# Loads of the row tiles of x issued from GpSimd's queue in a cumsum-difference matmul

## The chip, the cores and the metric

One Trainium2 chip, one core. The metric is device time in microseconds (us). Before: 1450.54 us, the median of three runs from 1450.36 to 1450.79.

## What is computed

The reference takes x (8 batches x 2048 rows x 2048 columns, float32) and w (2048 x 2048, float32):

```python
cs = np.cumsum(x, axis=1)
diff = cs - np.concatenate([np.zeros(...), cs[:, :-1, :]], axis=1)
return np.matmul(diff, w).astype(np.float32)
```

The difference of a running sum is the input again, so the kernel computes x @ w, with 16384 rows of x.

## The kernel before

The rows of x are cut into 128 tiles of 128 rows. The first four tiles ("plain", `PLAIN = 4`) are multiplied in bf16 in the ordinary way while w is still arriving. Their x comes in through `load_x` (L249), on SyncE's queue. From tile 4 on, tiles are taken four at a time: two pairs, and a scheme of Strassen's kind with fewer products, in f16. Each such group of four is one period of the program; after the first of these groups (`group_plain`) there are 30 periods of the same pattern (`group`).

A tile beyond the plain ones goes through these steps, each recorded by its own helper:

- `load` (L125): two halves of 512 KB each from x into one of four staging buffers F (`stage`, a list used first in, first out). The DMA is at L132.
- `weigh_one` (L135): ScalarE sums the absolute values of each half (L140), to get a scale.
- `scale_of` (L152): ScalarE adds the two sums (L161), VectorE takes the reciprocal (L163), ScalarE makes the unit that undoes the scale (L167).
- `narrow_one` (L173): ScalarE casts the half to f16 with that scale (L178). The narrowed second half gives its buffer back.
- `turn_one` (L193): a DMA transpose of each narrowed half into `turned_x` (L195). After the second one the other buffer is given back.
- Then TensorE multiplies (L588 in `matmuls`, L610 in `quarter`), ScalarE and VectorE empty PSUM (L624, L627, L635), VectorE forms sums of tiles and of blocks of w (L576), and SyncE stores (L643, L655).

Names in the text below are the kernel's own labels. `load0.0` is the first half of the first tile beyond the plain ones, `load2.0` and `load2.1` the halves of the third, and so on; `weigh0.0`, `narrow0.0` and `turn0.0` are the same half's later steps. A role from 4 to 10 names a tile that is prepared in one period for the next ones. The second of these tiles (`load1`) is loaded by a function of its own, `load_5`, at L517.

Before the products in f16 can start, w is scaled. VectorE takes the largest absolute value of every block of w (L305) and of all of these (L447); GpSimd takes the largest over the partitions (`max of all`, PARTITION_ALL_REDUCE, L451); from that come `uw` and `uinv` (L453, L454), and with them VectorE and ScalarE make the f16 blocks `B11`, `B21`, `B22` of w (L460, L462).

**The order is written out by hand.** Every operation is recorded with a label and the engine whose queue it goes to, and at the end `emit` (L205) sorts all of them by a number from the table `places`. `after` (L98) ties each operation behind the one before it on the same engine's list:

```python
def after(engine, ask):
    if engine in last:
        with tc.issue_after(last[engine].ins):
            said = ask()
    ...
    last[engine] = said[-1] if isinstance(said, tuple) else said
```

In `places`, `max of all` has number 235 and `load0.0` number 458. Before the change `max of all` is the only operation on the list "pool". SyncE's list "sp" has 817 DMAs: loads of x and w, transposes and stores.

Of the kernel before, what the change touches and what calls it, by code (L numbers as in the profile page):

```python
# [10 lines left out]
def kernel(  # L11
# [6 lines left out]
    nc = tc.nc  # L18
    P = 128
# [6 lines left out]
    NH = N // 2  # L26
# [21 lines left out]
    x2 = x.rearrange("b s d -> (b s) d")  # L48
# [67 lines left out]
    def record(label, engine, ask):  # L116
        at = seen[period[0], label] = seen.get((period[0], label), 0) + 1
        if at > 1:
            label = f"{label}#{at}"
        ops.append((period[0], label, engine, ask))  # L120

    def role(t):
        return t - PLAIN - 4 * period[0]

    def load(t, i):  # L125
        if t < END:
            to = stage.pop(0)
            where.setdefault(t, [None, None])[i] = to
            record(
                f"load{role(t)}.{i}",  # L130
                "sp",
                lambda: nc.sync.dma_start(to, x2[ds(t * P, P), ds(i * NH, NH)]),  # L132
            )

    def weigh_one(t, i):  # L135
# [308 lines left out]
    for t in (PLAIN, PLAIN + 2):  # L444
        load(t, 0)
        load(t, 1)
# [86 lines left out]
    narrow(PLAIN + 1)  # L533
    turn(PLAIN + 1)
    load(PLAIN + 3, 0)
    load(PLAIN + 3, 1)

# [1045 lines left out]
```

## Time and profile before

| what | us |
|---|---|
| median of three runs | 1450.54 |
| span of the profiled execution, first to last instruction | 1449.2 |
| TensorE (PE) busy in it | 1438.6 |
| VectorE (DVE) busy | 1334.3 |
| ScalarE (ACT) busy | 1204.5 |
| GpSimd (POOL) busy | 0.5 |

The profiled execution is known by its span of 1449.2 us; the median of the timed runs is 1.3 us above it, the time around the first and last instruction. The span is one execution on the one core. A busy share is the time in which the engine worked on an instruction; SyncE's queue only issues DMAs and is not counted. Its entries are written SPq. The time of a DMA "to landing" runs from the start of its issue to the update of its semaphore.

### The profile page before, as it was taken

What the parts mean: (1) busy time and instruction counts of PE and PEld (TensorE: products, weight loads), DVE (VectorE), ACT (ScalarE), POOL (GpSimd) and SP (SyncE); (2) the same over time, 40 slices, a digit from 0 to 9 for tenths busy, and PEclk for the clock granted to TensorE, in tenths of its full rate; (3) what the DMA queues carried; (4) which work ended last, traced back from release to release, by engine and by line L of the source; (5) the groups of instructions that cost most, each with busy time, mean ns of one, the idle gap of its engine ahead of it and who ended that gap; (6) DMA issues with size and microseconds to landing.
All of it is one profiled execution on the core that took longest, in us unless ns stands there. A gap on an engine that the chain in (4) does not pass through costs nothing.

```text
span 1449.2 us, 20358 instructions
## 1 busy us (share of the span) xinstructions
PE 1438.6 (99%) x6692; PEld 652.2 (45%) x6698; DVE 1334.3 (92%) x2345; ACT 1204.5 (83%) x1994; POOL 0.5 (0%) x5
## 2 busy tenths in 40 slices
PE   8999999999999999999999999999999999999998
PEld 4444444444444444444444444444444444444443
DVE  6999999999999999999999999999999999999988
ACT  5997888898888888888988888988888888889783
POOL 0000000000000000000000000000000000000000
PEclk9999999999999999999999999999999999999999
DMA  9999979899888999989998888998989998989973
GB/s 360 369 252 272 252 212 228 240 247 262 226 234 226 243 262 231 244 222 228 247 265 233 228 229 237 252 257 226 222 239 244 260 248 225 218 236 248 264 200 116
DMA packets 343930, 351.59 MB, mean 243 GB/s; under 512 B 270992, under 2 KB 270992, under 8 KB 343824
## 3 DMA queue, kind: packets, MB, share of 16 engines
q1 hardware_dynamic: 343824, 350.29, 89.4%
q8 instruction: 52, 0.85, 0.2%
q14 instruction: 54, 0.44, 0.1%
HBM read 150.99 MB, written 134.22 MB: 197 GB/s over the span
## 4 chain that ended last, share of the span: by engine, by line
PE 91%; issue 4%; DMA 2%; ACT 2%; DVE 1%; DVEq 0%; POOLq 0%; ACTq 0%; SPq 0%
PE b L610 61%; PE b L588 30%; DMA x<-F 1%; DMA F<-in_x_dram 1%; DVE W L460 1%; ACT waste L140 0%; DMA out_dram<-arena 0%; ACT W L462 0%; DVE arena L635 0%; ACT arena L624 0%; ACT F L178 0%; ACT arena L342 0%; ACT arena L178 0%; DVE arena L576 0%; DVE W L576 0%
## 5 line engine op out<-in xcount | busy, mean ns | idle before, releaser
L588 PE MATMUL b<-W,x 128*128 128x512 f16 x2144 | 518.1, 379 | 0.1
L635 DVE SCALAR_TENSOR_TENSOR arena<-b,tiny,arena 128x512 f32<-128x512 f32 x612 | 446.9, 745 | 16.0 <-PE b L610 4.8
L610 PEld LDWEIGHTS <-arena 128*128 128x128 f16 x2744 | 268.2, 98 | 325.4 <-DVE arena L576 6.3
L610 PE MATMUL b<-W,arena 128*128 128x512 f16 x1672 | 413.7, 379 | 0.8 <-DVE arena L576 0.4
L624 ACT ACTIVATE arena<-b,tiny 128x512 f32<-128x512 f32 x496 | 317.0, 684 | 35.4 <-PE b L588 14.9
L588 PEld LDWEIGHTS <-x 128*128 128x128 f16 x2144 | 209.7, 98 | 253.3 <-issue 0.3
L140 ACT ACTIVATE waste<-F,tiny 128x1024 uint8<-128x1024 f32 x246 | 283.9, 1154 | 15.6 <-DMA F<-in_x_dram 14.1
L178 ACT ACTIVATE F<-F,tiny 128x1024 f16<-128x1024 f32 x246 | 282.1, 1147 | 10.9 <-DVE tiny L163 9.4
L610 PE MATMUL b<-W,x 128*128 128x512 f16 x1192 | 287.5, 379 | 0.0
L610 PE MATMUL b<-arena 128*128 128x512 f16 x1072 | 261.6, 379 | 0.0
L610 PEld LDWEIGHTS <-x 128*128 128x128 f16 x1428 | 139.7, 98 | 168.5
L576 DVE TENSOR_TENSOR b<-b,arena 128x512 f32<-128x512 f32 x298 | 205.9, 691 | 5.7 <-ACT arena L627 2.0
L627 ACT COPY b<-b 128x512 f32<-128x512 f32 x149 | 85.5, 574 | 134.4 <-PE b L610 112.4
L627 ACT COPY arena<-b 128x512 f32<-128x512 f32 x298 | 170.2, 580 | 19.9 <-PE b L610 13.0
L576 DVE TENSOR_TENSOR arena<-W 128x2048 f16<-128x2048 f16 (+1 forms) x158 | 185.6, 1176 | 0.4 <-PE b L610 0.4
L576 DVE TENSOR_TENSOR arena<-x,x 128x512 f16<-128x512 f16 (+1 forms) x181 | 91.5, 506 | 50.1 <-PE b L610 50.1
L576 DVE TENSOR_TENSOR x<-x,x 128x1024 f16<-128x1024 f16 x124 | 85.2, 687 | 2.0
L576 DVE TENSOR_TENSOR arena<-W,arena 128x512 f16<-128x512 f16 (+1 forms) x157 | 85.9, 563 | 0.6 <-PE b L610 0.5
L576 DVE TENSOR_TENSOR arena<-arena 128x512 f16<-128x512 f16 x120 | 50.8, 424 | 13.7 <-PE b L610 11.8
L610 PE MATMUL b<-arena,x 128*128 128x512 f16 x236 | 60.3, 379 | 0.0
L324 PE MATMUL b<-arena 128*128 128x512 bf16 x234 | 53.5, 379 | 1.5 <-DVE arena L279 0.8
L576 DVE TENSOR_TENSOR arena<-x,arena 128x512 f16<-128x512 f16 x119 | 49.6, 417 | 0.6 <-PE b L610 0.6
(49 smaller groups left out, 503.6 us busy)
## 6 DMA issues: line engine op xcount, KB each, us to landing
F<-in_x_dram SPq DMA_DIRECT2D x246, 512.0 KB, 5.4
out_dram<-arena SPq DMA_DIRECT2D x240, 512.0 KB, 4.8
W<-in_w_dram SPq DMA_DIRECT2D x31, 512.0 KB, 9.5
out_dram<-arena SPq DMA_DIRECT2D x31, 256.0 KB, 2.7
W<-in_x_dram SPq DMA_DIRECT2D x16, 256.0 KB, 6.6
x<-F SPq DMA_TRANSPOSE x246, 4.4
arena<-in_x_dram SPq DMA_DIRECT2D x2, 512.0 KB, 5.1
W<-in_w_dram SPq DMA_DIRECT2D x2, 256.0 KB, 9.0
```

The source lines that it names most:

```text
L140: lambda: nc.scalar.activation(waste, data, ABS, bias=least, scale=1.0 / ROW, accum_out=m),
L178: lambda: nc.scalar.activation(to, data, COPY, scale=s),
L324: said = nc.tensor.matmul(to[n], xP[:, r, ko, :], b[:, ds(n * NB, NB)], start=(ko == 0), stop=(ko == KO - 1),)
L460: ask = lambda: nc.vector.tensor_scalar(to, src, uinv, None, MUL)
L576: record(label, "dve", lambda: nc.vector.tensor_tensor(dst, p, q, op))
L588: said = nc.tensor.matmul(to[n], a[k], b[k][:, n, :], start=(start and k == 0), stop=(k == KH - 1), skip_group_check=True,)
L610: said = nc.tensor.matmul(to, a[k], b[k], start=(start and k == 0), stop=(k == 3), skip_group_check=True)
L624: record(label, "act", lambda: nc.scalar.activation(c, p, COPY, scale=u))
L627: record(label, "act", lambda: nc.scalar.copy(to, p))
L635: label, "dve", lambda: nc.vector.scalar_tensor_tensor(c, p, u, c, MUL, ADD)
```

## The change

The loads at L132 are recorded for the list "pool" and issued with `nc.gpsimd.dma_start`. Source, destination, size and number (246, of 512 KB) stay. `load_x`, `load_5`, the loads of w, the transposes and the stores stay on SyncE's queue. The numbers in `places` stay as well, so on GpSimd's list the 246 loads stand behind `max of all`, in the order they had among themselves.

```diff
@@ -128,8 +128,8 @@
             where.setdefault(t, [None, None])[i] = to
             record(
                 f"load{role(t)}.{i}",
-                "sp",
-                lambda: nc.sync.dma_start(to, x2[ds(t * P, P), ds(i * NH, NH)]),
+                "pool",
+                lambda: nc.gpsimd.dma_start(to, x2[ds(t * P, P), ds(i * NH, NH)]),
             )
```

## Prediction

> **What bounds the kernel now.** I read the page first, for busy times and the chain that ended last, then the table of windows for one round of the loop, then the timelines of the place where the order of GpSimd's list touches the chain.
>
> ```profile
> PE 1438.6 (99%) x6692; PEld 652.2 (45%) x6698; DVE 1334.3 (92%) x2345; ACT 1204.5 (83%) x1994; POOL 0.5 (0%) x5
> PE 91%; issue 4%; DMA 2%; ACT 2%; DVE 1%; DVEq 0%; POOLq 0%; ACTq 0%; SPq 0%
> ```
>
> ```profile
> 386.40 12.09 PE b L610 x56
> ...
> 430.43 12.09 PE b L610 x56
> ```
>
> ```profile
> 711.00:755.00 44.00, 44.00 (x206) 19.94 (x204) 40.71 (x73) 37.45 (x64) 0.00 (x0) 1.00 0.92 239
> ```
>
> The second block is the chain in order of time: the same piece returns after 430.43 - 386.40 = 44.03 us. The third is the windows table (PE, PEld, DVE, ACT, POOL busy with counts, clock, DMA share, GB/s). TensorE is busy for all 44.00 us of a round at the full clock, and has the same matmuls to do after the change. So the loop can't get shorter. Loads can only cost, where TensorE is made to wait.
>
> **The change part by part: SyncE's side.** What goes is 246 issues.
>
> ```profile
> L132 SPq DMA_DIRECT2D F<-in_x_dram x246: 327/524/2110, 49.5 to 1396.0; - x123
> DMA to landing us min/median/max: 3.0/4.9/9.7
> ```
>
> 246 x 0.524 = 129 us of SyncE's queue go. I count them at nothing: TensorE, idle for 0.00 us of the round, hides them. Stores and transposes may be issued up to about half a microsecond earlier, and nothing on the chain waits for that.
>
> **The loop.** A load on GpSimd's queue waits for its staging buffer alone, and behind it stand only later loads. Here is the tightest half-tile of a round, `load7.0`, and the next, `load7.1`: SyncE's timeline, then ScalarE's, then the landing of the transpose at 768.89, of the load at 775.80 and of the load at 778.33.
>
> ```profile
> 768.89 1.24 SPq L195 DMA_TRANSPOSE x<-F  x1
> ...
> 775.80 0.38 SPq L132 DMA_DIRECT2D F<-in_x_dram  x1
> ...
> 778.33 0.34 SPq L132 DMA_DIRECT2D F<-in_x_dram  x1
> ```
>
> ```profile
> 781.66 1.15 ACT L140 ACTIVATE waste<-F,tiny 128x1024 uint8<-128x1024 f32 x1 [0.96 <-DMA F<-in_x_dram]
> ...
> 785.78 1.15 ACT L140 ACTIVATE waste<-F,tiny 128x1024 uint8<-128x1024 f32 x1
> ```
>
> ```profile
> DMA to landing us min/median/max: 3.3/3.3/3.3
> ```
>
> ```profile
> DMA to landing us min/median/max: 5.8/5.8/5.8
> ```
>
> ```profile
> DMA to landing us min/median/max: 5.6/5.6/5.6
> ```
>
> `load7.0` lands at 775.80 + 5.8 = 781.6 and ScalarE has waited 0.96 us for it: no margin. But its buffer came free when the transpose (`turn4.1`) landed, at 768.89 + 3.3 = 772.2; it then stood 3.6 us in SyncE's order. On GpSimd's queue it can go 3.6 us earlier. `load7.1` was issued as its buffer came free; it lands at 778.33 + 5.6 = 783.9, 1.9 us ahead of its use. Behind it comes its transpose, the second of these two (landing row of that one second), and VectorE's sum that reads it:
>
> ```profile
> 789.08 3.66 SPq L195 DMA_TRANSPOSE x<-F  x2
> ...
> 798.00 0.68 DVE L576 TENSOR_TENSOR arena<-x,x 128x1024 f16<-128x1024 f16 x1
> ```
>
> ```profile
> DMA to landing us min/median/max: 5.0/5.2/5.4
> ```
>
> No transpose of the two started after 790.5 (the second took the last 2.3 of the 3.66 us), so it lands by 795.9, at least 2.1 us ahead of the sum. A load issued by GpSimd may thus land 1.9 + 2.1 = 4.0 us later than one issued by SyncE before the round grows. The trace shows no DMA issued by GpSimd. I bound the difference by a gain of 1.9 us (the landing's median 4.9 against its minimum 3.0: a load no longer stands behind stores and transposes in one queue) and a loss of 4.8 us (maximum 9.7 against the median). I take a loss of 0.5 us, one more issue at SyncE's median. In the loop that costs nothing.
>
> **The start: here the order changes.** GpSimd's list has `max of all` ahead of `load0.0`, and it runs in order.
>
> ```profile
> 60.20 0.35 POOL L451 PARTITION_ALL_REDUCE tiny<-tiny  x1 [59.77 <-DVE tiny L447]
> ```
>
> ```profile
> L132 SPq DMA_DIRECT2D F<-in_x_dram x4: 327/328/328, 49.5 to 54.1; - x4
> ...
> DMA to landing us min/median/max: 9.6/9.6/9.7
> ```
>
> ```profile
> 58.61 1.04 ACT L313 CAST arena<-W 128x1024 bf16<-128x1024 f32 x1
> 59.56 1.14 ACT L140 ACTIVATE waste<-F,tiny 128x1024 uint8<-128x1024 f32 x1
> ...
> 62.10 0.29 ACT L161 ACTIVATE tiny<-tiny 128x1 f32<-128x1 f32 x1
> ```
>
> ```profile
> 61.04 2.74 DVE L460 TENSOR_SCALAR W<-W,tiny 128x1024 f16<-128x1024 f32 x4
> 63.70 0.16 DVE L163 RECIPROCAL tiny<-tiny 128x1 f32<-128x1 f32 x1
> 63.77 4.71 DVE L460 TENSOR_SCALAR W<-W,tiny 128x1024 f16<-128x1024 f32 x7
> ...
> 68.47 4.05 DVE L460 TENSOR_SCALAR W<-W,tiny 128x1024 f16<-128x1024 f32 x6
> ```
>
> ```profile
> 69.07 0.81 PE L476 MATMUL b<-W,arena 128*128 128x512 f16 x3
> 69.72 0.59 PE L324 MATMUL b<-arena 128*128 128x512 bf16 x2
> 70.15 2.75 PE L588 MATMUL b<-W,x 128*128 128x512 f16 x12
> ```
>
> Now the first load is issued at 49.5 and lands at 59.1; ScalarE starts `weigh0.0` at 59.56 straight after its last cast. After the change the reduction, which waits for VectorE until 60.20, holds the loads back to 60.20 + 0.35 = 60.55. So:
>
> 1. `load0.0` lands at 60.55 + 4.9 (median landing) + 0.5 = 65.95, and `weigh0.0` starts there: D = 65.95 - 59.56 = 6.4 us late.
> 2. `mean0` (L161) ended at 62.39, and VectorE's `scale0` (L163) came at 63.70 because VectorE was busy until then: 1.3 us of slack. So `scale0` and the blocks of w behind it in VectorE's order move by 6.4 - 1.3 = 5.1 us.
> 3. TensorE's first product in f16, `left over.0` at 69.07, needs `B11.6`, the last of the seven at 63.77, at 68.48: now 73.6, a wait of 4.5 us. Then come 5 matmuls, and the first product of group 0 at 70.15, whose third matmul (70.15 + 2 x 0.23 = 70.6) needs `B11.2`, the third of the six at 68.47, done at 68.47 + 3 x 0.675 = 70.5: now 75.6. Together TensorE stands about 5.1 us longer.
>
> The other condition of that product is `turn0.0`:
>
> ```profile
> 63.89 1.15 ACT L178 ACTIVATE F<-F,tiny 128x1024 f16<-128x1024 f32 x1 [0.18 <-DVE tiny L163]
> ```
>
> ScalarE waited 0.18 us for VectorE there, so `turn0.0` moves by 6.2 us; issued after the cast's end at 65.04 with the 3.3 us that transposes took above, it landed near 68.4, 1.8 us early, and now binds 4.4 us. `B11.2` ends last. The other three loads need to follow each at 1.3 us, ScalarE's pace (59.56 to 62.10 is two of them); 512 KB at the 403 to 407 GB/s of this stretch take 1.3 us, so they just do:
>
> ```profile
> 60.20:63.70 3.50, 3.50 (x17) 1.59 (x17) 2.98 (x7) 3.44 (x8) 0.35 (x1) 1.00 1.04 403
> ```
>
> Nothing gives the 5.1 us back, as TensorE has no idle time after it in the loop. **Sum:** the span goes from 1449.2 to 1454.3; with the 1.3 us that the median of 1450.54 lies above the span, **1455.6 us**. Bounds of step 1: landing in 3.0 us gives D = 4.0 and a stall of 2.7 us, 1453.2; landing in 9.7 us gives D = 10.7 and 9.4 us, 1459.9.
>
> **The rivals.** *The clock falls during the stall.* At both ends of the kernel TensorE stands idle:
>
> ```profile
> 1444.20:1447.60 3.40, 0.00 (x0) 0.00 (x0) 1.45 (x3) 0.00 (x0) 0.00 (x0) 1.00 0.86 308
> 1447.60:1449.20 1.60, 0.00 (x0) 0.00 (x0) 0.00 (x0) 0.00 (x0) 0.00 (x0) 0.53 0.00 0
> ...
> 1.20:3.80 2.60, 2.60 (x7) 0.95 (x8) 1.91 (x7) 0.80 (x1) 0.00 (x0) 1.00 0.59 154
> 3.90:7.40 3.50, 3.50 (x17) 1.37 (x14) 0.00 (x0) 0.00 (x0) 0.00 (x0) 1.00 0.90 269
> ```
>
> About 3.4 us after the last matmul the clock was at half, and at the start 7 matmuls took the 2.60 us in which a running array does 2.60 / 0.206 = 12.6. A wait of 4.5 us could do the same once: (12.6 - 7) x 0.206 = 1.2 us, 1456.8. Against it: the one idle stretch in the trace that let the clock fall was about as long as this one. The Trainium skill (TensorE: Matmul & The Clock Gate, Part 1) says that one idle window of about 3.4 us, free-running, halves the clock; by that an idle of 4.5 us holds a full window only sometimes.
>
> *GpSimd can't write its descriptors while VectorE scales w.*
>
> ```profile
> L635 DVE SCALAR_TENSOR_TENSOR arena<-b,tiny,arena 128x512 f32<-128x512 f32 x612 | 446.9, 745 | 16.0 <-PE b L610 4.8
> ```
>
> VectorE runs TENSOR_SCALARs without a gap from 61.04 to 61.04 + 2.74 = 63.78, then stands until the load is there. If GpSimd is held until then, `load0.0` lands at 63.78 + 5.4 = 69.2, D = 9.6, the stall is 8.3, and with the clock's 1.2 the time is 1458.8 to 1460.0. For it: 1024 f32 in 2.74 / 4 = 0.69 us is double the pace of the 512 in 0.745 us of the sums from PSUM quoted here, so a special mode. Against it: GpSimd's first issue can begin at 60.55, ahead of 61.04. The Trainium skill (SBUF — State Buffer, Who interferes with whom) states this lock for such modes, and infers that TENSOR_TENSORs with two inputs, of which the loop has many, don't hold descriptors up; no run here shows either.
>
> *The loop grows.* If GpSimd's loads land more than 4.0 us later, or its packets, now in a queue of their own, delay the last transpose by over 2.1 us, each of 30 rounds grows by the excess: 0.3 us gives 9 more, 1464.6; 1 us gives 1485.6. For it: VectorE is idle for 44.00 - 40.71 = 3.3 us of a round, little if GpSimd needs that time. Against it: the 4.0 us and the 3.6 us that the tightest load gains.
>
> *Not slower.* The first loads have idle DMA queues: w has come, and the stores are out sooner. If `load0.0` lands within 60.55 + 3.2 = 63.75, the stall is at most 2.9 us; at the minimum of 3.0 us it is 1453.2, within 0.2% (2.9 us, about what a measurement of this kernel can tell from no change). That is where it decides. A second way is that the loads don't in fact wait behind the reduction: then `weigh0.0` starts at 59.6 as now, 1450.5. I give that little, as `after` ties them.
>
> **How the numbers follow.** Stall without a fall of the clock (1453.5 to 1458.5): 0.34, my forecast 1455.6. With the fall: 0.20. Held descriptors: 0.17. Loop grows: 0.14. Not slower: 0.15, of which 0.02 faster by over 0.2%. So slower 0.85, same 0.13, faster 0.02. The range 1452.8 to 1466 leaves out most of the grown loop and the second way of the last rival, under 0.2.
>
> **What would show it.** In the profile after: the first GpSimd load starts near 60.6 and lands near 66; `weigh0.0` (ACT L140) starts there after a wait for the DMA of some 6 us; VectorE waits some 5 us ahead of L163; TensorE's gap is near 69 to 76, and the chain's pieces still return every 44.03 us. A period over 44.03, or ScalarE waiting at L140 in each round, would prove the loop rival; a first landing before 63.8 the last one; a low clock after 73 the first.

## The result, and the profile after

| | us |
|---|---|
| before, median of 6 runs (1449.31 to 1450.79) | 1450.36 |
| after, median of 6 runs (1598.12 to 1640.75) | 1621.77 |
| the profiled execution after | 1605.0 |
| its span | 1603.2 |
| after over before | 1.109 [1.1052, 1.1128] |

The ratio is taken from the three runs of after that lie within 1.5% of its fastest (1598.12, 1605.0 and 1621.35). In the profiled execution the change costs about 155 us, over the six runs 148 to 190, where 5.1 were forecast. The forecast was right in the sign and wrong in the size: the result lies far above its range.

The page of the kernel after, with busy times, the two DMA queues and the shares of the chain that ended last:

```profile
span 1603.2 us, 20778 instructions
...
PE 1484.8 (93%) x6698; PEld 654.0 (41%) x6698; DVE 1337.7 (83%) x2345; ACT 1204.8 (75%) x1994; POOL 131.2 (8%) x251
...
q1 hardware_dynamic: 308400, 221.30, 60.5%
q0 software_dynamic: 35424, 128.99, 32.7%
...
PE 45%; DMA 34%; DVE 11%; ACT 6%; issue 3%; SPq 0%; POOL 0%; DVEq 0%; POOLq 0%; ACTq 0%
```

TensorE had 91% of the chain before; now it has 45%, and DMAs have 34%. TensorE is idle for 1603.2 - 1484.8 = 118 us, where it was idle for 10.6; that is 108 of the 154 us by which the span grew. The other 46 us are busy time (1484.8 against 1438.6), with the same matmuls to do. The mean granted clock of this execution is 0.978, where it was 0.999, and by an estimate from these, 1603.2 x 0.021 = 34 of the 46 us are the slower clock; the gap at the start, below, shows such a fall behind a wait. The loads have moved to a queue of their own (q0).

Pieces of that chain in order of time (start, length, what):

```profile
630.07 12.09 PE b L610 x56
674.12 12.25 PE b L610 x56
...
1456.91 17.13 DMA x<-F
```

Some rounds still take 674.12 - 630.07 = 44.05 us, the length of before. Others contain a transpose (`x<-F`) as a link of the chain, mostly of 8 to 17 us, and they are longer; the longest round takes 56 us. `DMA x<-F` has 17% of this chain, where it had 1% before, near the loop's start. The stores (`DMA out_dram<-arena`) have 9%, where they had less than 1%.

The transposes' own rows, of before and then of after (issue time min/median/max in ns; who waited for them; time to landing):

```profile
L195 SPq DMA_TRANSPOSE x<-F x246: 1231/1282/5393, 65.1 to 1407.6; - x123
...
DMA to landing us min/median/max: 3.0/4.4/8.6
```

```profile
  POOL F L132: 800.8, 97
  DVE arena L576: 61.8, 28
...
DMA to landing us min/median/max: 3.0/5.8/17.1
```

Before, nobody waited for a transpose. After, VectorE's sums waited 28 times, 61.8 us in all, and the longest landing is 17.1 us where it was 8.6. The loads' own row of after:

```profile
L132 POOL DMA_DIRECT2D F<-in_x_dram x246: 527/527/957, 61.0 to 1550.0; - x123
...
DMA to landing us min/median/max: 3.9/6.3/17.2
```

The waits of after (who, for what: us in all, times, longest):

```profile
PEld L610 <- DVE arena L576: 68.2, 58, 5.2
ACT waste L140 <- DMA F<-in_x_dram: 61.3, 29, 6.1
DVE tiny L163 <- ACT tiny L161: 58.0, 52, 6.0
DVE arena L576 <- DMA x<-F: 54.6, 27, 4.5
...
ACT arena L624 <- DMA out_dram<-arena: 40.3, 43, 3.2
```

Three paths lead to TensorE. A late transpose holds VectorE's sum (L576), which holds TensorE. A late load holds ScalarE (L140), then VectorE's reciprocal (L163), and both engines run in order. A late store, which stands in SyncE's queue with the transposes, holds the result buffer that ScalarE needs to empty PSUM (L624); before, this cost 4.9 us in 4 waits. The stores' median landing rose from 4.8 to 6.4 us.

**One jam, read closely.** SyncE's and then GpSimd's timeline of after around 1360, the landing of `turn5.1` (issued at 1346.96, ahead of these rows), that of the two transposes shown, and the windows row of the middle of it:

```profile
1357.20 5.48 SPq L195 DMA_TRANSPOSE x<-F  x2
```

```profile
1360.02 1.05 POOL L132 DMA_DIRECT2D F<-in_x_dram  x2 [12.24 <-DMA x<-F]
```

```profile
DMA to landing us min/median/max: 12.5/12.5/12.5
```

```profile
DMA to landing us min/median/max: 6.6/10.1/13.5
```

```profile
1364.00:1370.00 6.00, 4.88 (x23) 1.98 (x21) 4.08 (x6) 2.08 (x4) 0.00 (x0) 1.00 1.07 90
```

Two transposes (`turn7.0`, `turn7.1`) are issued at 1357.2 and 1359.0. Two loads (`load8.1`, `load10.0`) start at 1360.02 in the other queue, while these transposes are under way. In the order of before, `load8.1` stood ahead of both in the one queue and `load10.0` behind both. `load8.1` is late because GpSimd waited 12.24 us for the buffer that `turn5.1` gives back, and `turn5.1` had taken 12.5 us beside `load8.0`, issued 0.3 us after it. So one late transpose pushes the next load onto the next transposes. The second transpose lands 13.5 us after its issue. In the middle, packets are under way on the DMA engines all the time (share 1.07) and move 90 GB/s; before, a round averaged 239 at a share of 0.92. A share over 1 shows that packet times of the two queues overlap, so they include waiting.

**The start** went much as the prediction had it. GpSimd's timeline, then ScalarE's, VectorE's and TensorE's, all of after:

```profile
60.73 0.35 POOL L451 PARTITION_ALL_REDUCE tiny<-tiny  x1 [60.29 <-DVE tiny L447]
60.95 2.82 POOL L132 DMA_DIRECT2D F<-in_x_dram  x4
```

```profile
65.20 1.15 ACT L140 ACTIVATE waste<-F,tiny 128x1024 uint8<-128x1024 f32 x1 [5.01 <-DMA F<-in_x_dram]
...
74.07 1.05 ACT L342 COPY arena<-b 128x512 f32<-128x512 f32 x2
```

```profile
61.58 2.74 DVE L460 TENSOR_SCALAR W<-W,tiny 128x1024 f16<-128x1024 f32 x4
68.20 0.16 DVE L163 RECIPROCAL tiny<-tiny 128x1 f32<-128x1 f32 x1 [3.88 <-ACT tiny L161]
68.28 4.71 DVE L460 TENSOR_SCALAR W<-W,tiny 128x1024 f16<-128x1024 f32 x7
```

```profile
75.17 1.44 PE L476 MATMUL b<-W,arena 128*128 128x512 f16 x3 [5.41 <-ACT arena L342]
```

The first load waits for the reduction, ScalarE for the load, VectorE for ScalarE, and TensorE stands for 5.41 us. Its next three matmuls take 1.44 us, where they took 0.81 before: the clock fell. The granted clock was 0.50 from 75 to 80 us, where it was 1.00 before.

### The profile page after: what moved, and what is told of

The parts are those of the page before. It is cut to its first block, busy times and chain, and to the rows that moved or that the text cites. A ratio compares the mean times of both kernels' runs of the same rounds, so it can differ in the third digit from the quotient of the medians.

```text
span 1603.2 us, 20778 instructions
## 1 busy us (share of the span) xinstructions
PE 1484.8 (93%) x6698; PEld 654.0 (41%) x6698; DVE 1337.7 (83%) x2345; ACT 1204.8 (75%) x1994; POOL 131.2 (8%) x251
## 2 busy tenths in 40 slices
DMA packets 343933, 351.61 MB, mean 219 GB/s; under 512 B 270992, under 2 KB 270992, under 8 KB 343824
## 4 chain that ended last, share of the span: by engine, by line
PE 45%; DMA 34%; DVE 11%; ACT 6%; issue 3%; SPq 0%; POOL 0%; DVEq 0%; POOLq 0%; ACTq 0%
PE b L610 30%; DMA x<-F 17%; PE b L588 15%; DMA out_dram<-arena 9%; DMA F<-in_x_dram 6%; DVE arena L635 5%; DVE arena L576 3%; ACT F L178 2%; DMA W<-in_w_dram 2%; ACT arena L624 1%; DVE tiny L305 1%; DMA x<-arena 1%; ACT waste L140 1%; ACT arena L627 1%; DVE b L576 1%
## 5 line engine op out<-in xcount | busy, mean ns | idle before, releaser
L610 PE MATMUL b<-W,arena 128*128 128x512 f16 x1672 | 435.3, 392 | 80.5 <-DVE arena L576 42.4
L624 ACT ACTIVATE arena<-b,tiny 128x512 f32<-128x512 f32 x496 | 319.2, 683 | 78.5 <-DMA out_dram<-arena 40.3
L140 ACT ACTIVATE waste<-F,tiny 128x1024 uint8<-128x1024 f32 x246 | 284.1, 1155 | 61.9 <-DMA F<-in_x_dram 61.3
L178 ACT ACTIVATE F<-F,tiny 128x1024 f16<-128x1024 f32 x246 | 281.8, 1145 | 16.7 <-DVE tiny L163 15.4
L132 POOL DMA_DIRECT2D F<-in_x_dram x246 | 130.8, 532 | 1358.8 <-DMA x<-F 783.7
L576 DVE TENSOR_TENSOR b<-b,arena 128x512 f32<-128x512 f32 x298 | 205.9, 691 | 23.4 <-ACT arena L627 20.7
L576 DVE TENSOR_TENSOR arena<-W 128x2048 f16<-128x2048 f16 (+1 forms) x158 | 185.6, 1176 | 1.0 <-PE b L610 0.7
L576 DVE TENSOR_TENSOR arena<-x,x 128x512 f16<-128x512 f16 (+1 forms) x181 | 92.1, 509 | 111.8 <-DMA x<-F 54.6
L576 DVE TENSOR_TENSOR x<-x,x 128x1024 f16<-128x1024 f16 x124 | 85.2, 687 | 2.0
L576 DVE TENSOR_TENSOR arena<-W,arena 128x512 f16<-128x512 f16 (+1 forms) x157 | 85.9, 563 | 0.6 <-PE b L610 0.5
L576 DVE TENSOR_TENSOR arena<-arena 128x512 f16<-128x512 f16 x120 | 50.7, 423 | 25.2 <-PE b L610 23.3
L163 DVE RECIPROCAL tiny<-tiny 128x1 f32<-128x1 f32 x124 | 20.1, 162 | 58.5 <-ACT tiny L161 58.0
```

Of the source, the lines that this page charges most:

```text
L132: lambda: nc.gpsimd.dma_start(to, x2[ds(t * P, P), ds(i * NH, NH)]),
L140: lambda: nc.scalar.activation(waste, data, ABS, bias=least, scale=1.0 / ROW, accum_out=m),
L163: record(f"scale{role(t)}", "dve", lambda: nc.vector.reciprocal(s, m))
L178: lambda: nc.scalar.activation(to, data, COPY, scale=s),
L576: record(label, "dve", lambda: nc.vector.tensor_tensor(dst, p, q, op))
L610: said = nc.tensor.matmul(to, a[k], b[k], start=(start and k == 0), stop=(k == 3), skip_group_check=True)
```

## The experiments

The theories, by the letters that some expectations use. A: a transpose beside loads of another queue makes the DMA engines lose throughput as such. B: the loads that GpSimd issues land late by themselves. C: the two queues share the engines fairly. D: the engines take packets in turn from the two queues, and a transpose, of many small packets, is pushed behind the loads. E: it is the transposing itself that comes out badly beside loads, not the size of the packets. The rivals besides: the start explains all, or the loads themselves come too late.

### The two halves of the change: the first four loads, and all others

```diff
-                "sp",
-                lambda: nc.sync.dma_start(to, x2[ds(t * P, P), ds(i * NH, NH)]),
+                "pool" if t in (PLAIN, PLAIN + 2) else "sp",
+                lambda on=(nc.gpsimd if t in (PLAIN, PLAIN + 2) else nc.sync): on.dma_start(
+                    to, x2[ds(t * P, P), ds(i * NH, NH)]),
```

> Only the first four loads are on GpSimd's queue, the other 242 on SyncE's. All theories agree on the mechanism (behind the reduction they start at 60.7 and TensorE stands about 5 us, and the clock falls once): 1455 to 1460 us. If the first group of the kernel after the change lost its 35 us through these four loads and not through later ones, it is 1470 or more.

Measured: 1458.42 us (1456.79 to 1460.02), 1.0061 [1.0044, 1.0078]. TensorE's timeline:

```profile
74.67 1.44 PE L476 MATMUL b<-W,arena 128*128 128x512 f16 x3 [5.94 <-ACT arena L342]
75.91 1.06 PE L324 MATMUL b<-arena 128*128 128x512 bf16 x2
76.76 3.20 PE L588 MATMUL b<-W,x 128*128 128x512 f16 x12
```

The start alone costs about 8 us. A gap of 5.94 us, and (1.44 - 0.81) + (1.06 - 0.59) + (3.20 - 2.75) = 1.55 us of slower matmuls against the same rows of before, make 7.5 us at that place. The profiled execution is the fastest of the four; its span is 1455.0, 5.8 above before's, so some of this is won back later.

The other half has `not in` in the place of `in`:

> The other part alone: the first four loads stay on SyncE's queue, the other 242 go to GpSimd's. Theory A (collisions in the loop): the loss is here, 1580 to 1630 us, and rounds of 44.03 us stand beside rounds of 50 us and more. If the late start throws the loop out of step, so that it is the cause of the long rounds, the loop returns to 44.03 us and the time to under 1460.

Measured: 1570.71 us in the profiled execution, 1570.71 to 1612.78 in four runs, without the start's delay; 1580 to 1630 were expected, and three of the four lie there. So most of the loss isn't in the first four loads. The transposes' landing there:

```profile
DMA to landing us min/median/max: 3.0/5.5/16.9
```

How much lies in the loop can be read at one instruction. Every trace of the whole kernel has the same 2345 instructions of VectorE in the same order; this is the sum at the end of the loop's first round, before and after:

```profile
177.68 0.68 DVE L576 TENSOR_TENSOR arena<-x,x 128x1024 f16<-128x1024 f16 x1
```

```profile
200.68 0.68 DVE L576 TENSOR_TENSOR arena<-x,x 128x1024 f16<-128x1024 f16 x1
```

After is 23.0 us late there and 1603.2 - 1449.2 = 154 us late at its end. So 131 us are lost in the 29 rounds that follow, 4.5 a round, and 23 us ahead of them. With the first four loads alone on GpSimd's queue this sum comes at 182.90, 5.2 us late; the rest of the 23 us comes with the other loads of the first group, whose transposes `turn0.1` and `turn1.1` landed after 12.2 and 13.6 us beside loads.

### The transposes replaced by plain copies

The same bytes go from and to the same places on SyncE's queue, with all loads on GpSimd's; only the order inside a tile is not turned. First in rows of 2 KB:

```diff
-        record(f"turn{role(t)}.{i}", "sp", lambda: nc.sync.dma_start_transpose(to, data))
+        record(f"turn{role(t)}.{i}", "sp", lambda: nc.sync.dma_start(
+            to.rearrange("p k m -> p (k m)"), data))
```

> As the kernel after the change, all 246 loads on GpSimd's queue, but the DMA transposes are plain copies of the same 256 KB within SBUF; the tiles are not transposed, so the products are those of other matrices. Theory A (transpose against load): the rounds return to 44.03 us and the time is 1452 to 1462, what the late start costs. Theory B (GpSimd's loads land too late by themselves, or their descriptors wait for VectorE): rounds stay at 49 us or so and the time over 1550.

Measured: 1458.03 us (1456.43 to 1458.48), 1.0052 [1.0036, 1.0068]. That is the start's cost and nothing more: the loop's loss is gone though all loads are in the second queue. But the copies also have fewer packets. So the next kernel cuts each into pieces of 256 bytes, two DMAs of 128 KB for one transpose (part of the edit):

```diff
+        rows = data.rearrange("p (k m) -> p k m", k=KH)
+            lambda: [
+                nc.sync.dma_start(to[:, k::2, :], rows[:, k::2, :]) for k in range(2)
+            ][-1],
```

> As the kernel after the change, all loads on GpSimd's queue, with each transpose replaced by plain copies of the same bytes in 256-byte pieces (two DMAs of 512 pieces each; the tiles are not transposed, so other products). If small packets against large ones in another queue are the cause (theory D), it is as slow as the kernel after the change, over 1540 us. If the transposing itself is (theory E), the loop returns to 44.03 us and the time to about 1458 us, as with copies of whole rows.

Measured: 1459.76 us (1458.09 to 1460.08), 1.0062 [1.0039, 1.0085]. The page's packet count is 343940, against 343933 in the kernel after:

```profile
DMA packets 343940, 351.66 MB, mean 241 GB/s; under 512 B 270993, under 2 KB 270993, under 8 KB 343825
```

and the pieces land in

```profile
DMA to landing us min/median/max: 2.2/4.6/8.2
```

As many small packets as before, in the same two queues, and none of the 17 us landings. That speaks against D as the whole cause and for E. It isn't a pure test: the copies are issued in two steps, and their page shows a lower DMA share in the loop (7 to 8 tenths) than that of after (mostly 9). Before the change the share of a round was 0.92 already, so these two runs don't separate something peculiar to transposing from the DMA time that it takes.

### What the queues do alone

A kernel of DMAs only: 12 transposes, 12 loads of 512 KB, 12 plain copies and 12 stores, in one queue and in two, each group after the last has landed.

```python
for i in range(N):    # N = 12
    after("pool", lambda: nc.gpsimd.dma_start(loaded[i], x2[ds(i * P, P), ds(0, 1024)]))
    after("sp", lambda: nc.sync.dma_start_transpose(turned[i], src))
gate()                # all have landed before the next group
```

> A kernel of DMAs alone: eleven stretches one after the other, each of 12 transposes of 256 KB, 12 loads or 12 stores of 512 KB, or two of these kinds together, on the queues named. It computes nothing of the reference. Theory A (transposes and loads collide when they are in flight in two queues): transposes and loads together on SyncE's queue take about the sum of the two alone (some 12 x 1.7 and 12 x 1.4, near 38 us), while transposes on SyncE with loads on GpSimd take far more, over 60 us; loads on GpSimd alone as long as on SyncE alone; copies in place of the transposes bring the stretch back to the sum. If the second queue matters and not that software fills it, loads on ScalarE's queue are as slow as on GpSimd's. Theory B (loads issued by GpSimd are slow by themselves): loads on GpSimd alone take longer than on SyncE alone, and the pair is no slower than the sum. Theory C (the two queues share fairly): transposes with loads on GpSimd take the sum, as on one queue.

Measured, from first issue to last landing, in us:

| 12 of each | us |
|---|---|
| transposes on SyncE | 18.8 |
| loads on SyncE / on GpSimd | 19.1 / 19.7 |
| both on SyncE | 37.1 |
| transposes on SyncE, loads on GpSimd (twice) | 34.4, 32.9 |
| transposes on SyncE, loads on ScalarE | 44.8 |
| copies on SyncE, loads on GpSimd | 28.8 |
| transposes on SyncE, stores on GpSimd / on ScalarE | 34.9 / 38.6 |
| stores on SyncE, loads on GpSimd | 35.3 |

Theory A falls for GpSimd: two queues are not slower in all. But the order inside is another. The windows (VectorE and GpSimd busy, clock, DMA share, GB/s) of the transposes beside GpSimd's loads:

```profile
119.00:134.00 15.00, 0.72 (x5) 2.12 (x4) 1.00 1.04 392
134.00:147.00 13.00, 2.30 (x18) 0.00 (x0) 1.00 1.05 203
```

The loads run at nearly their own speed first; the transposes follow. The packets of each queue from 120 to 133:

```profile
q0 software_dynamic: 1336, 4.84, 94.1%
q1 hardware_dynamic: 1267, 0.32, 10.9%
```

and, for the transposes alone, from 18 to 34:

```profile
q1 hardware_dynamic: 11716, 2.91, 103.6%
```

Alone, transposes send 11716 / 16 = 732 packets per us; beside loads 1267 / 13 = 97, one for each of the loads' 1336 / 13 = 103. The Trainium skill (DMA: Bandwidth & Descriptors, Queues, rings and completion order) says that each DMA engine goes round between queues packet by packet; the nearly equal counts of this trace agree. The pieces above, as many packets without that loss, suggest that it isn't enough for the kernel's loss.

### One or two of each

The kernel's situation is two transposes and one to three loads. A second kernel of DMAs times small groups:

```python
load(0); load(1)     # GpSimd's queue
turn(0); turn(1)     # SyncE's queue
gate()               # all have landed before the next group
```

> DMAs alone again, as in the first such kernel (nothing of the reference is computed), but only one or two transposes beside one to three loads, as they meet in the loop; thirteen stretches, three times over. Theory D (the DMA engines take one packet of each queue in turn, and a transpose of 256-byte packets pays a 4 KB packet for each of its own while loads last): a transpose alone lands in about 3.2 us; every load in the other queue adds its own 1.3 us to it, so 4.5 with one, 5.8 with two; two transposes beside two loads land some 6 and 8 us after the issue; copies of whole rows hardly suffer. Theory E (there is a jam beyond fair turns, as the packet times of over 1 us in the loop suggest): beside two loads the second transpose lands later than 9 us and the loads, too, take longer than the 5.7 us that two of them take alone. The stretch with loads and transposes all on SyncE's queue shows the sum in both.

Measured, landing after the group's first issue, three repetitions:

| group | transposes | loads |
|---|---|---|
| two transposes | 3.2, 4.5 | |
| one transpose, one load on GpSimd | 5.9 to 6.2 | 5.6 to 5.9 |
| one transpose, two loads on GpSimd | 7.1 to 7.7 | 5.6 to 6.0, 7.3 to 7.6 |
| two transposes, two loads on GpSimd | 6.8 to 7.1, 8.3 to 8.7 | 5.8 to 5.9, 7.4 to 7.8 |
| two transposes, three loads on GpSimd | 7.5 to 7.8, 10.3 to 10.4 | 5.7 to 5.9, 8.0 to 8.1, 9.4 to 9.6 |
| SyncE alone: two transposes, then two loads | 3.2 to 3.3, 4.4 to 4.5 | 6.7 to 7.2, 7.9 to 8.9 |
| SyncE alone: two loads, then two transposes | 6.7 to 6.9, 7.7 to 7.8 | 3.9 to 4.1, 5.6 to 5.9 |
| two copies in 256-byte pieces, two loads on GpSimd | (copies) the last at 7.7 to 7.8 | 4.4 to 4.7, 6.5 to 6.6 |

The landing row, from each one's own issue, of two transposes beside two GpSimd loads:

```profile
DMA to landing us min/median/max: 7.1/7.1/7.1
```

This is the heart of it. In SyncE's queue a transpose issued ahead of a load goes through ahead of it, in 3.2 us. With the load in another queue the transpose lands between the two loads or with the last, after 7.1 us, as late as behind two loads in SyncE's queue. (In SyncE's queue the first load is issued 2.7 us after the first transpose, here 0.2 us after it; the order and the later start go together.) D put the two transposes at some 6 and 8 us, E the second beyond 9; they landed at 7 and 8.5. The pieces also land late here, at 7.7 against 4.3 to 4.4 alone, so these small groups don't tell D from E, and 7 us are not yet 13.

> DMAs alone (nothing of the reference is computed): one to four transposes on SyncE's queue, with or without two stores behind them, and two loads on GpSimd's queue at once or about 1 us later, or on ScalarE's. If the transfers only share the engines, the last of each set lands within 1 us of the sum of its parts (two transposes 4.4 us, two loads 1.3 each more: about 8 us), with GpSimd's and ScalarE's queue alike. If there is a jam as in the loop (90 GB/s for 6 us with the engines busy), some set lands 3 us or more after that sum, most likely one with more than two transposes or with stores.

The third kernel adds the stores that stand around the transposes in the loop. Its issues (median us to landing), first two transposes and two stores alone, then with two GpSimd loads about 1 us later:

```profile
out_dram<-kept SPq DMA_DIRECT2D x2, 512.0 KB, 3.4
t<-src SPq DMA_TRANSPOSE x2, 3.2
```

```profile
l<-in_x_dram POOLq DMA_DIRECT2D x2, 512.0 KB, 6.3
out_dram<-kept SPq DMA_DIRECT2D x2, 512.0 KB, 8.2
t<-src SPq DMA_TRANSPOSE x2, 6.5
```

The group ends at 11.8 to 12.4 us, 2.3 to 2.9 us beyond the transposes and stores alone (about 6.9) and two loads (2.6 more, at the 1.3 us that a second load adds). That is just short of the 3 us that were to mark a jam. Without the stores, and the loads about 1 us later, the second transpose lands at 8.5 to 9.0, where it lands at 4.5 alone. With one store ahead and two loads beside it, a transpose issued 0.4 us in lands at 9.4 to 9.9: 9 us for what takes 3.2 alone (the store ahead without the loads was not run). With the loads on ScalarE's queue, two transposes that alone land at 3.2 and 4.5 land at 6.5 to 7.7 and 7.4 to 8.5: a second queue delays them, whoever issues. The 13.5 us of the kernel are reached in part only.

### Which loads

```diff
+                "pool" if period[0] > 0 and role(t) < 8 else "sp",
```

> All loads of the first group on SyncE's queue; in the loop five of eight on GpSimd's (roles 5, 6 and 7), three on SyncE's (roles 8 and 10). The transposes that landed latest in the kernel after the change are turn5.1 and turn7.1; beside them stood load7.1 and load8.0, and load8.1 and load10.0. Theories D and E: only turn5.1 still meets a load of the other queue, so most of the loss goes: 1452 to 1490 us. If each load on GpSimd's queue costs the same wherever it stands, five eighths of the loop's loss remain: about 1545 us.

> The other part: in the loop the three loads of roles 8 and 10 are on GpSimd's queue, the five of roles 5, 6 and 7 on SyncE's. Theories D and E: turn7.1 meets load8.1 and load10.0, turn5.1 meets load8.0: most of the loss stays, 1520 to 1600 us. If each load costs the same, three eighths stay: about 1505 us.

The first keeps the loads of roles 8 and up on SyncE's queue, the second those below 8 (`>= 8` in place of `< 8`); in both, `period[0] > 0` keeps the whole first group there. Measured: 1454.58 us (1451.04 to 1460.98), 1.0032 [1.0011, 1.0052], and 1490.89 us (1490.65 to 1491.14), 1.0279 [1.0249, 1.0309]. The first came as expected. The second was a miss: a loss, but 40 us, not the 70 or more expected. Its wait for loads:

```profile
ACT waste L140 <- DMA F<-in_x_dram: 57.4, 46, 4.8
```

Here it is ScalarE's waiting for late loads; VectorE waited for transposes only five times. And 4 + 40 = 44 us are a third of the 131 that the loop loses when both sets are on GpSimd's queue. The two sets of loads cost more together than apart.

### The loads made to follow the transposes

All loads on GpSimd's queue, but in the loop those of roles 8 and 10 wait, by a semaphore, until the transpose that stands ahead of them in SyncE's order has landed. This takes the overlap with these transposes away and leaves the queue. (Part of the edit; the helper `behind` adds the dependency on the last transpose issued.)

```diff
+                lambda late=(period[0] > 0 and role(t) >= 8): behind(
+                    nc.gpsimd.dma_start(to, x2[ds(t * P, P), ds(i * NH, NH)]), late
+                ),
```

> As the kernel after the change, but in the loop the loads of roles 8 and 10 wait for the landing of the transpose that stood ahead of them in SyncE's order (load8.0 for turn5.1, load10.0 for turn7.1). The transfer and the queue are the same, only the overlap with these two transposes goes. If the overlap is the cause, most of the loop's loss of about 150 us goes: 1455 to 1500 us, and turn5.1 and turn7.1 land in some 6 us again. If GpSimd's queue costs by itself, the later start makes it no better than the kernel after the change: 1600 us or more.

Measured: 1478.8 us (1474.46 to 1483.15), 1.0197 [1.0126, 1.0269], as expected for the overlap. The transposes land in

```profile
DMA to landing us min/median/max: 3.0/5.0/13.0
```

and `turn5.1` and `turn7.1` land in 6.1 and 4.7 us in the median, where after had 11.4 and 11.6. The sum at the end of the loop's first round:

```profile
194.39 0.68 DVE L594 TENSOR_TENSOR arena<-x,x 128x1024 f16<-128x1024 f16 x1
```

This kernel is 16.7 us late there, against 177.68, and 1472.7 - 1449.2 = 23.5 us late at its end. So most of what is left was lost in the first group, where no load waits. Of the loop's 131 us, 6.8 are left in the profiled execution, though these loads have one more thing to wait for. What costs most is that loads run beside transposes, and neither that GpSimd issues them nor that they are late.

### Another queue, and another transfer in the second queue

```diff
-                "sp",
-                lambda: nc.sync.dma_start(to, x2[ds(t * P, P), ds(i * NH, NH)]),
+                "act",
+                lambda: nc.scalar.dma_start(to, x2[ds(t * P, P), ds(i * NH, NH)]),
```

> As the kernel after the change, but the 246 loads are issued from ScalarE's queue, which is filled by hardware as SyncE's is. If any second queue beside the transposes does the harm, the transposes' landing again rises from 4.4 to about 6 us and the time is over 1540 us (ScalarE also waits in its own order for free buffers, so it can be worse than GpSimd's). If only GpSimd's software-filled queue does, the transposes land in 4.4 us as before, and what is lost is ScalarE's waiting alone: the loads' share of issues, some 8 x 0.5 us a round, has room beside 37.5 us of work, 1450 to 1500 us.

Measured: 1600.23 us (1598.14 to 1602.32), 1.1035 [1.1, 1.107]. That is as slow as after, but by another wait:

```profile
ACT waste L140 <- DMA F<-in_x_dram: 138.6, 98, 4.9
```

The transposes' median landing is 4.8 us, between the 4.4 and the 6 of the two forecasts. Most of the loss is ScalarE's own order, in which a load's issue stands among its casts and copies. So in place this run settles nothing about the queue; the group of two transposes beside ScalarE's loads above does, alone.

```diff
-                "sp",
-                lambda: nc.sync.dma_start(out2[ds(t * P, P), ds(h * NH, NH)], c),
+                "pool",
+                lambda: nc.gpsimd.dma_start(out2[ds(t * P, P), ds(h * NH, NH)], c),
```

> The kernel before, with the 512 KB stores of the loop on GpSimd's queue in place of the loads (all loads and transposes on SyncE's). If any large transfer in a second queue beside the transposes does the harm, the transposes land later than 4.4 us in the median and the time is 1480 to 1620 us. If it is loads into SBUF that collide with the transposes' writes into SBUF, the stores do little: under 1460 us.

Here the loads are back on SyncE's queue and the 512 KB stores go from GpSimd's. Measured: 1460.77 us (1459.42 to 1462.12), 1.0073 [1.0044, 1.0102], with the transposes at

```profile
DMA to landing us min/median/max: 3.0/4.7/7.8
```

That lies between the two forecasts, next to the 1460 us of the second. Stores in a second queue, nearly as many bytes as the loads, cost 10 us, not 155. A second queue beside transposes is not fatal in itself; with loads that come in just behind the transposes it is.

## Why the prediction was wrong, step by step

- **The bound** was right. The loop was at TensorE's limit, the change could only cost, and it did.
- **The start, step 1**, was right: `load0.0` was put at 60.55 and landing at 65.95; it was issued at 60.95 (the reduction itself came 0.5 us later) and ScalarE began at 65.20. The median landing of 4.9 us that was added there came from a row that mixed loads with transposes; the loads' own row before was 3.7/5.4/9.7. The first one took 4.2, so the slip cost nothing.
- **The other three loads** were not quite in time: they "just do" in the prediction, but ScalarE waited 1.04 us for the third.
- **Step 2** was right: `scale0` and the seven blocks behind it came at 68.20 and 68.28, 4.5 later than before; 5.1 were forecast.
- **Step 3** named the wrong last condition. TensorE's wait ends with ScalarE's copies (L342), which stand behind two sums and two casts in ScalarE's order and moved from 67.44 to 74.07; the block of w was done earlier, at 68.28 + 4.71 = 72.99. So the product came at 75.17, not 73.6, and the gap is 5.41 us, not 4.5. That the start's sum came out near is in part luck, as the load came 0.75 us sooner and TensorE's last condition 1.6 us later than the sum had them. "Nothing gives the 5.1 us back" was too strong: with the first four loads alone, 7.5 us at the start were 5.8 at the end of the profiled execution.
- **The clock** fell at the start, as the rival "with the fall" had it: 1.55 us with the first four loads alone, 1.2 forecast. The start's 8 us against the rival's 6.3 is a fair size. What no rival had is the slower clock behind the loop's waits (0.98 from 160 to 1560 us), most of the 34 us estimated above.
- **Held descriptors** fell as a rival. GpSimd's first issue took 0.69 us though it began at 60.95, ahead of VectorE's TENSOR_SCALARs; the three that ran beside these, from 61.58, took 0.67 to 0.81, against a median of 0.527. The Trainium skill (SBUF — State Buffer, Who interferes with whom) states an exclusive lock for such modes; here, at most some 0.3 us per issue of it can be seen.
- **The tightest load** gained, as forecast. In medians over the rounds, `load7.0` lands 2.45 us ahead of its use, where it had 0.02.
- **The step that failed is "In the loop that costs nothing".** It priced a load that lands 0.5 us later, and its median is 0.9 later; that was nearly right and beside the point. It left out of the sum what the change does to the transposes that stay. The rival "Loop grows" named this ("its packets, now in a queue of their own, delay the last transpose by over 2.1 us") and got 0.14, against which stood the 4.0 us of margin and the 3.6 us that the tightest load gains. But the gain is the harm: the loads went earlier because they no longer stood behind the transposes, and so ran beside them. `load8.0` started 4.5 us after `turn5.1` before and 0.3 us after it now, `load10.0` 2.4 us after `turn7.1` and now 0.45. In medians over the 25 rounds whose order is the same, `turn5.1` landed 5.84 us after its issue before and 11.43 after; its margin to VectorE's sum fell from 4.44 to 0.09 us. `turn7.1` went from 4.40 to 11.63 us, its margin from 3.16 to 0.14. By the rival's own rule, 131 us over 29 rounds are an excess of 4.5 us a round, where its examples were 0.3 and 1.
- **What could have been read before:** SyncE's queue was priced as a wait of the loads (3.6 us) and not as a shelter of the transposes. The prediction's `turn4.1` landed in 3.3 us with loads due behind it, and the DMA share of a round, 0.92, stood in its windows row.

What is shown: 131 of the 154 us are lost in the loop (the sum at its first round), the loss goes when plain copies take the transposes' place (copies, pieces), it needs loads at the same time as the transposes (the run with the waits), and a transpose alone in its queue loses its lead over loads of another (the small groups). What stays open: whether it is the transposing as such or the DMA time that it takes; why the engines now and then move only 90 GB/s, which the small groups give in part; why the two sets of loads cost more together than apart; and why stores beside transposes cost so much less. No version beat the kernel before, whose loop leaves TensorE no idle time to win back.

## What to carry to other kernels

An order in one DMA queue can be more than issue time: here it kept short, urgent transfers ahead of long ones behind them, and moving the long ones to another queue took that away. Before moving a transfer, list what it used to stand behind, and ask what those transfers' readers can bear if they land only when the moved ones do. Where transposes are among them, keep the loads in their queue, or move them only if they can be made to start after the transposes have landed.

## What the hardware showed that was not expected

In the jam from 1364 to 1370 the packets themselves are slow. The queues of after in this stretch:

```profile
q0 software_dynamic: 104, 0.39, 79.4%
q1 hardware_dynamic: 230, 0.13, 26.7%
```

A load's packet took 0.794 x 16 x 6 / 104 = 0.73 us from its start to its end; in the first DMA-only kernel, from 120 to 133, it took 0.941 x 16 x 13 / 1336 = 0.15. That is five times as long at nearly the same share of the engines (1.06 and 1.05), so taking turns alone doesn't give it. Stores stand in SyncE's queue here too; what slows the packets, no run shows.

GpSimd's issue of a 512 KB load took 0.527 us, nearly SyncE's 0.524, and alone it landed in 3.9 to 4.3 us. The issuing engine as such costs nothing here. The Trainium skill (DMA: Bandwidth & Descriptors, Issuing engines are not separate DMA queues) has all issuers' DMAs interleave on the same engines; the traces agree, and in this kernel leaving the one queue cost 10.9%.

With the loads on ScalarE's queue, 12 transposes and 12 loads took 44.8 us, against 37.1 in one queue and 34.4 with GpSimd's: who issues in the second queue does matter for the total.
